# Attention beside a stream of products: factors turned behind the weighted sums, used behind the next minima; operand pieces split a visit after their load

## The chip, the cores and the metric

The kernel runs on one core of a Trainium2 chip. Its metric is the device time in microseconds of one execution of the whole program, from a launch to its end. TensorE (PE) multiplies and turns matrices into PSUM, VectorE (DVE) and ScalarE (ACT) work on tiles elementwise, GpSimd (POOL) does a few elementwise operations and issues stores, and SyncE (SP) issues most of the loads. Each of these runs its own list of instructions in order, and they wait for one another by semaphores.

## The reference, cut to what matters

One decoder layer on 1024 tokens of width 1024, in float32: two branches, a state space model (ssm) and an attention with forgetting, are gated, merged and projected. The part around the change is the attention of 16 heads of 64 columns, and the branch products behind it:

```python
scale = ATT_HEAD_DIM ** -0.5
fcum = jnp.cumsum(log_f, axis=-1)
for blk in range(seqlen // ATT_BLOCK):
    q0, q1 = blk * ATT_BLOCK, (blk + 1) * ATT_BLOCK
    s = jnp.einsum('bhqd,bhkd->bhqk', q[:, :, q0:q1], k[:, :, :q1]).astype(jnp.float32) * scale
    s = s + fcum[:, :, q0:q1, None] - fcum[:, :, None, :q1]
    s = jnp.where(kpos[None, :] <= qpos[:, None], s, -jnp.inf)
    prob = jax.nn.softmax(s, axis=-1)
    outs.append(jnp.einsum('bhqk,bhkd->bhqd', prob.astype(v.dtype), v[:, :, :q1]))
...
y_att = (o.astype(f32) * jax.nn.silu(z_att.astype(f32))).astype(x.dtype)
p_ssm = jnp.einsum('ble,ed->bld', y_ssm, w_branch_ssm)
p_att = jnp.einsum('ble,ed->bld', y_att, w_branch_att)
merged = jax.nn.sigmoid(g_ssm) * p_ssm + jax.nn.sigmoid(g_att) * p_att
out = jnp.einsum('bld,de->ble', merged, w_out)
return x + _rmsnorm(out, post_g)
```

## The kernel before

**The stream of products.** Every large product is a `Pair`: two units of 128 output columns computed by a scheme of seven block products (`do`, numbers 1 to 7). Each block product is one *step* of 12 matmuls (`matmuls`, four pieces of 128 rows by three products of high and low parts) and runs in two halves of six. `Stream.steps` is a list of all steps written out by hand; `half` runs the next half, and three steps ahead prepares the weights' high and low part (`split` in `Pair`: ACT writes the high part, L351, DVE the low part, L352; the tile is `wop`). The results go from PSUM (`pb`, `pc`, `pd`) to SBUF by `keep` (L404) and `give` (L412 to L418).

**Operands.** The moving side of a product is an operand of four pieces, each 128 x 512, in a high and a low part (`x0h`, `x0l` and so on; x0 is `b11`, x1 `b21`, x2 `-b22`, x3 `t1`, x4 `-t2`, x5 `t3`, x6 `t4`). Three sets follow one another in the same tiles: the layer's input at first, then the ssm branch's output (`ops_s`), the attention's output (`ops_a`), and in the end the output weights (`ops_w`). Where a pair is the last that uses a set, each operand is opened for the next set as soon as its step is over (`Stream.half`), and `Operands.some`, called once a half, does two things: it fetches up to two pieces that are ready (L265, SP loads), and it splits up to two pieces that were fetched more than two calls ago (ACT L277 or L280, DVE L278 or L281, both held to the program's order). With a name given (`only`), at a step's start, it splits what that step still lacks. During the second part of a visit's fill the calls are put off (`hold`) and done one after another in the next visit (`release`).

**Attention.** It runs beside the stream in 48 visits, six a pair of heads (`GROUPS`): two query blocks against up to 512 keys. A visit m of the loop from L1599 does, in order:

- `scores`: the products on PE into four score tiles (`s`, one for each head and block), for each a minimum on DVE (L1459, tile `ex`, minimum `nm`) and an exponential with its sum on ACT (L1463), held to this order;
- `weighted`, of the visit before: the weighted sums (`av`) on PE;
- every second visit `free`, which multiplies the sums of the group just ended by its gate and frees the PSUM bank (`o`, L1412);
- `release`, then at a group's end `settle`, which compares the minima of the key halves;
- `fill(m, 0)`: halves of the stream's steps, a share worked out from `rooms` and `weights`;
- at a group's end `scale`, which makes eight factors a query (`ns`), and `load_gates`; `loads` of queries, keys, values and gates for later visits;
- `turned`: the exponentials turned on PE into `pt` and copied to `p` by ACT or DVE;
- `fill(m, 1)`, with the operands' calls put off.

A group of query blocks ends every second visit (g odd; n = 0, 1, 2 in a pair of heads). Its factors lie one query to a row and have to be turned: `send` turns them on PE (`tp`), copies them on ACT (`st`, L1385) and has POOL store them to DRAM in two pieces (`st_dram`, L1387); `take` loads them back with two SP loads, spread over the rows (`rb`, L1393); `out` multiplies by them on DVE (L1424 and the addition L1425, or L1418 alone for n = 2) and calls `outputs`, which has POOL store the result (`ya_dram`, L1514) and make the differences that the scheme of seven needs.

Before the change, a group that ends in visit m is sent in visit m + 1 behind `turned`, taken at the start of visit m + 2 ahead of `fill(m + 2, 0)`, and put out in visit m + 2 behind `turned`. For the last pair of heads, groups 1 and 2 were taken at the end of visit m + 1 and put out ahead of that fill.

**What sets the order.** All of PE's instructions stand as the program has them (`mm`, `turn`), and so do those marked `pin` on the other engines, among them the minima, the exponentials, the operands' splits, the multiplications by factors and POOL's stores. All others, the loads on SP too, are placed among these by a planner that goes by its own estimate of the durations; those under `tc.high_priority()` come first when they can. The score tiles, `pt` and `tp` are all of one tag with four PSUM banks, used in turn: a new tile takes the bank of the fourth last and waits for whoever still reads that.

Of the kernel before, what the change touches and what calls it, by code (L numbers as in the profile page):

```python
# [19 lines left out]
NK = D // P  # L20
# [66 lines left out]
def hybrid_layer(ctx: ExitStack, tc, a, out):  # L87
# [73 lines left out]
    class Operands:  # L161
# [9 lines left out]
        def __init__(self, name, src, there=lambda k, h: True, order=lambda op: op, queue=nc.gpsimd):  # L171
            self.src, self.there, self.order, self.queue = src, there, order, queue
            self.copy = src
            self.tiles, self.left, self.made, self.at, self.step = {}, {}, set(), {}, 0
            self.lows = {}
            self.dram = {n: tc.dram_tile([KH, P, HALF], F32, name=f"{n}_{name}") for n in self.LESS}

# [111 lines left out]
        def put(self, j, **parts):  # L289
            for name, raw in parts.items():  # L290
                self.made.add((name, j))
                name = "-" + name if name in ("t2", "b22") else name
                self.at[name, j] = self.step
                self.split(name, j, raw)

        def some(self, only=None):

            self.step += 1
            n = 0
            for name in list(self.left):  # L300
                for j in list(self.left[name]):
                    if (only is None and n < 2 or name == only) and (name, j) not in self.at:
                        if self.ready(name.strip("-"), j):
                            self.fetch(name, j)
                            self.at[name, j] = self.step
                            n += 1
            n, most = 0, 1 if "merged" in fin else 2
            for name, j in list(self.at):
                if j in self.left[name]:
                    if name == only or only is None and n < most and self.at[name, j] < self.step - 2:  # L310
                        self.split(name, j)
                        n += 1

# [142 lines left out]
    class Stream:  # L456
# [6 lines left out]
        def __init__(self, pairs, double, last):  # L463
            self.pairs = pairs
            for n, p in enumerate(pairs):
                p.bank, p.other = (pj, "be"[n % 2]), (pjx, "d") if n < double else (pj, "c")

                p.between = n < double or n >= last

            p, q, r = pairs[0:3]  # L470
            self.steps = [(p, 1), (q, 1), (p, 2), (q, 2)] + [(p, n) for n in (6, 5, 7, 3, 4)]
            self.steps += [(q, 6), (q, 5), (q, 7), (r, 1), (q, 4), (q, 3)]
            for n in range(2, last):
                p, nxt = pairs[n], pairs[n + 1]
                self.steps += [(p, i) for i in ((2, 6, 5, 7) if n < double else (6, 2, 7, 5))] + [(nxt, 1)]
                self.steps += [(p, 4), (p, 3)] if n + 1 < last else [(p, 3), (p, 4)]

            a, b, c, d, e, f, g, h = pairs[last:]
            self.steps += [(a, 5), (a, 6), (a, 7), (b, 1), (a, 2), (a, 4), (a, 3)]
            for p, nxt in ((b, c), (c, d), (d, e)):  # L480
                self.steps += [(p, 2), (p, 6), (p, 5), (p, 7), (nxt, 1), (p, 4), (p, 3)]
            self.steps += [(f, 1), (e, 2), (e, 6), (e, 5), (e, 7), (f, 2), (e, 4), (e, 3)]
            self.steps += [(f, 6), (f, 5), (f, 7), (g, 1), (f, 4), (f, 3)]
            self.steps += [(g, 2), (g, 6), (g, 5), (g, 7), (h, 1), (g, 4), (g, 3)]
            self.steps += [(h, 6), (h, 5), (h, 7), (h, 2), (h, 3), (h, 4)]
            self.following = {p: n.ops for p, n in zip(pairs, pairs[1:]) if n.ops is not p.ops}
            self.building = []
            self.chores = []
            self.held = None
            self.count = 0  # L490
            self.at = 0
            self.run = None
            self.waiting = []
            self.loads = [(p, names) for p in pairs for names in (("a11", "a12"), ("a21", "a22"))]
            self.loaded = []
            self.load_next()
# [635 lines left out]
    with tc.tile_pool(name="pro", bufs=1, reuse_waits="tile", side="right") as pro, tc.tile_pool(  # L1132
        name="prop", bufs=1, space=PSUM, reuse_waits="tile", side="right"
# [51 lines left out]
        stream = Stream(order + late + ends, len(order) + 1, len(order) + len(late) + 4)  # L1185
# [58 lines left out]
    with tc.tile_pool(name="ssm", bufs=1, reuse_waits="tile", side="right") as sp, tc.tile_pool(  # L1244
        name="ssmp", bufs=1, space=PSUM, reuse_waits="tile", side="right"
# [42 lines left out]
    with tc.tile_pool(name="att", bufs=1, reuse_waits="tile", side="right") as ap, tc.tile_pool(  # L1288
        name="attp", bufs=1, space=PSUM, reuse_waits="tile", side="right"
# [139 lines left out]
        heads = {}  # L1429
# [162 lines left out]
        def fill(m, part):  # L1592
            share = weights[min(m // 6, NK - 1)] * rooms[m % 6][part]
            to = stream.steps.index((ends[4], 6))
            stream.halves(round((2 * (to - stream.at) - (stream.run is not None)) * share / left[0]))
            left[0] -= share

        made = []
        for m in range(6 * NK + 1):  # L1599

            hp, g = divmod(m, 6)
            if not g and hp < NK:
                heads[hp] = Heads(hp)
            if m < 6 * NK:
                for u in range(2):
                    scores(hp, g, u)
            for one in made:
                weighted(*one)
            for hd, which in end(m - 1):
                hd.free(which)  # L1610
            stream.release()
            if m == 6 * NK:
                heads[NK - 1].out(2)
                break
            for hd, which in end(m):
                hd.settle(which)
            for hd, which in end(m - 2):
                if not hd.last or not which:
                    hd.take(which)
                else:  # L1620
                    hd.out(which)
            fill(m, 0)

            for hd, which in end(m):
                hd.scale(which)
                hd.load_gates(which)
            loads(m)
            made = turned(hp, g)
            for hd, which in end(m - 2):
                if not hd.last or not which:  # L1630
                    hd.out(which)
            for hd, which in end(m - 1):
                hd.send(which)
            if m == 6 * NK - 1:
                heads[hp].send(2)
            stream.hold()
            fill(m, 1)
            for hd, which in end(m if m == 6 * NK - 1 else m - 1):
                if hd.last and which:
                    hd.take(which)  # L1640


    fp = ctx.enter_context(tc.tile_pool(name="fin", bufs=1, reuse_waits="tile", side="right"))
# [56 lines left out]
```

## Time and profile before

| | |
|---|---|
| time, median of 3 runs | 1315.51 us (1313.98 to 1316.69) |
| the profiled execution's own time | 1316.03 us |
| its span, first to last instruction | 1314.3 us |
| mean granted clock of TensorE | 0.990 |
| attention stage in the span, scores of the first to the sums of the last visit | about 673 to 1158 us |
| operands of the ssm branch loaded and split | about 934 to 1003 us |
| operands of the attention branch loaded and split, as far as in the attention stage | from about 1096 us |

The profile is one execution as the hardware recorded it. A group of instructions is told by its line, its engine and the names that it writes and reads (`out<-in`), with count, total busy time, mean duration, and the time for which the engine stood idle just before, with what ended that. In a timeline each row has start, duration, engine, line and names; an idle time of the engine just before stands in brackets with its releaser. PEclk is the share of its full clock that TensorE was granted. Where a helper records all matmuls they share the line L130 and all transpositions L133; tiles tell them apart.

### The profile page before, as it was taken

How to read it: one execution, taken by the hardware profiler on the slowest of the kernel's cores; microseconds unless marked ns; L12 is line 12 of the kernel's file. 1: busy time of each engine (PE TensorE's matmuls, PEld its weight loads, DVE VectorE, ACT ScalarE, POOL GpSimd, SP SyncE). 2: the span in 40 equal slices, each digit the busy share in tenths (PEclk: the TensorE clock that was granted, in tenths of full speed). 3: DMA queues.
4: the chain of work that ended last, by engine and by line, in shares of the span. 5: the costliest groups of instructions: out<-in, count | busy, mean ns of one | idle time of the engine just before them, and what ended most of it. 6: DMA issues, size and time to landing. Idle time of an engine off the chain costs nothing.

```text
span 1314.3 us, 21050 instructions
## 1 busy us (share of the span) xinstructions
PE 1264.7 (96%) x7054; PEld 992.0 (75%) x7054; DVE 1017.0 (77%) x1977; ACT 793.3 (60%) x1726; POOL 304.0 (23%) x311
## 2 busy tenths in 40 slices
PE   5899999999999999899999999999989998999997
PEld 4578888788887788688777777777767776678886
DVE  7988888798789879778667667666778666888975
ACT  7645665567556656566556565666667555644754
POOL 4000340024102420133002122222121222346152
PEclk9999999999999999999999999999989998999999
DMA  8232543545364545444564657565677556756933
GB/s 292 60 124 65 157 142 121 197 136 154 125 192 124 147 159 158 125 149 153 169 241 157 208 193 228 194 200 195 215 253 264 193 188 216 235 187 214 366 110 104
DMA packets 154668, 233.59 MB, mean 178 GB/s; under 512 B 17216, under 2 KB 62656, under 8 KB 154560
## 3 DMA queue, kind: packets, MB, share of 16 engines
q1 hardware_dynamic: 142016, 205.53, 48.8%
q0 software_dynamic: 6400, 16.10, 3.2%
q10 hardware_dynamic: 6144, 10.62, 2.1%
q8 instruction: 55, 0.90, 0.3%
q14 instruction: 53, 0.43, 0.1%
HBM read 162.99 MB, written 72.34 MB: 179 GB/s over the span
## 4 chain that ended last, share of the span: by engine, by line
PE 70%; DVE 10%; DMA 7%; ACT 6%; issue 4%; SPq 1%; POOL 0%; ACTq 0%; DVEq 0%
PE pb L130 29%; PE pc L130 16%; PE pd L130 5%; PE av L130 5%; PE s L130 5%; PE pt L133 4%; PE yps L130 2%; DVE wop L352 2%; DMA raw<-in_wu 2%; ACT wop L351 1%; PE tr L133 1%; ACT ex L1463 1%; DVE sum L357 1%; PE st L130 1%; DMA xt<-in_x 1%
## 5 line engine op out<-in xcount | busy, mean ns | idle before, releaser
L352 DVE TENSOR_TENSOR wop<-sum,wop 128x512 fp32r<-128x512 f32 x178 | 143.3, 805 | 56.5 <-ACT wop L351 56.2
L1463 ACT ACTIVATE ex<-ex,nm 128x512 f32<-128x512 f32 (+1 forms) x192 | 116.1, 606 | 91.8 <-DVE nm L1459 90.5
L351 ACT ACTIVATE wop<-sum 128x512 fp32r<-128x512 f32 x178 | 111.3, 626 | 94.8 <-PE pc L130 38.8
L404 ACT ACTIVATE s<-pb 128x512 f32<-128x512 f32 x144 | 85.3, 593 | 105.0 <-PE pb L130 101.2
L130 PE MATMUL pc<-x3h,wop 128*128 128x512 f32 x384 | 131.1, 399 | 2.1 <-ACT wop L351 1.0
L352 DVE TENSOR_TENSOR wop<-raw,wop 128x512 fp32r<-128x512 f32 x146 | 106.8, 733 | 33.4 <-ACT wop L351 33.1
L130 PE MATMUL pb<-x6h,wop 128*128 128x512 f32 x384 | 131.0, 398 | 1.2 <-ACT s L404 1.2
L130 PE MATMUL pb<-x0h,wop 128*128 128x512 f32 x384 | 131.8, 401 | 0.0
L130 PE MATMUL pb<-x4h,wop 128*128 128x512 f32 x384 | 130.3, 396 | 0.8 <-ACT x4h L1178 0.8
L130 PE MATMUL pc<-x2h,wop 128*128 128x512 f32 x384 | 130.4, 398 | 0.1
L130 PE MATMUL pb<-x5h,wop 128*128 128x512 f32 x384 | 129.3, 395 | 0.8 <-ACT s L404 0.7
L1459 DVE CUSTOM_DVE_ANT_0 ex<-s,fb 128x512 f32<-128x512 f32 (+1 forms) x192 | 96.7, 551 | 23.3 <-PE s L130 23.3
L351 ACT ACTIVATE wop<-raw 128x512 fp32r<-128x512 f32 x146 | 90.7, 623 | 15.9 <-PE pc L130 9.9
L130 PE MATMUL pd<-x1h,wop 128*128 128x512 f32 x272 | 91.2, 394 | 0.0
L130 PEld LDWEIGHTS pc<-x3h,wop 128*128 128x128 f32 x384 | 72.8, 190 | 20.8 <-issue 4.2
L213 POOL TENSOR_TENSOR wd<-wd 128x256 f32<-128x256 f32 x32 | 33.3, 1040 | 229.1 <-DMA wd<-in_wo 106.5
L130 PEld LDWEIGHTS pb<-x6h,wop 128*128 128x128 f32 x384 | 72.6, 189 | 18.1 <-ACT s L404 1.7
L130 PEld LDWEIGHTS pb<-x0h,wop 128*128 128x128 f32 x384 | 73.4, 191 | 17.0 <-issue 1.8
L130 PEld LDWEIGHTS pb<-x4h,wop 128*128 128x128 f32 x384 | 72.2, 188 | 18.2 <-issue 2.4
L130 PEld LDWEIGHTS pb<-x5h,wop 128*128 128x128 f32 x384 | 72.1, 188 | 18.1 <-ACT s L404 1.7
L130 PEld LDWEIGHTS pc<-x2h,wop 128*128 128x128 f32 x384 | 72.1, 188 | 17.5 <-issue 2.1
L130 PE MATMUL s<-k,q 64*128 64x512 f32 (+3 forms) x576 | 76.0, 378 | 5.8 <-ACT p L1483 3.3
(310 smaller groups left out, 3006.4 us busy)
## 6 DMA issues: line engine op xcount, KB each, us to landing
raw<-in_wu SPq DMA_DIRECT2D x128, 256.0 KB, 3.7
csb<-cs_dram SPq DMA_DIRECT2D x32, 256.0 KB, 5.0
fb<-f_dram SPq DMA_DIRECT2D x16, 512.0 KB, 6.3
rb<-st_dram SPq DMA_DIRECT2D x48, 128.0 KB, 3.1
wd<-in_wo SPq DMA_DIRECT2D x40, 128.0 KB, 3.2
xt<-in_x SPq DMA_DIRECT2D x8, 512.0 KB, 5.9
gs_dram<-th ACTq DMA_DIRECT2D x16, 256.0 KB, 2.6
qh_dram<-th SPq DMA_DIRECT2D x16, 256.0 KB, 4.9
```

The costliest lines, as they stand in the source:

```text
L130: return tc.keep_in_program_order(nc.tensor.matmul(*args, **kw))
L133: return tc.keep_in_program_order(nc.tensor.transpose(out_, in_, idn))
L213: pin(nc.gpsimd.tensor_tensor(t[out_], t[a_], t[b_], ALU.subtract))
L351: nc.scalar.activation(op[:, 0], src, AF.Copy)
L352: nc.vector.tensor_tensor(op[:, 1], src, op[:, 0], ALU.subtract)
L357: self.adds.tensor_tensor(t, x, y, ALU.add)
L404: nc.scalar.activation(s, ps, AF.Copy)
L1459: nc.vector.tensor_tensor_reduce(o, s[e][:, 0:w], fb[hp, h][:, e, 0:w], 1.0, 3.0e38, ALU.add, ALU.min, nm)
L1463: pin(nc.scalar.activation(o, o, AF.Exp, scale=-1.0, bias=nm, accum_out=hd.at(hd.sm, i, h, e)))
```

## The change

- `send` goes from behind `turned` to behind the weighted sums of the same visit, right after `free`, so on PE the factors' transposition stands behind the last weighted sums of its group.
- `take` goes from the start of visit m + 2 to visit m + 1, behind `turned` and ahead of `fill(m + 1, 1)`.
- `out` goes from behind `turned` of visit m + 2 to behind the scores, minima and exponentials of that visit, ahead of the weighted sums.
- The last pair of heads is no longer treated apart, but for its group 2, which is sent and taken in visit 47 and put out in visit 48 as before.
- The stream knows the number of the visit (0 outside the attention). `Operands.some` splits a fetched piece only in a later visit than that of its fetch, except at the start of the step that needs it.

```diff
@@ class Operands, put
-                self.at[name, j] = self.step
+                self.at[name, j], self.visit[name, j] = self.step, stream.visit
                 self.split(name, j, raw)
@@ class Operands, some
                             self.fetch(name, j)
-                            self.at[name, j] = self.step
+                            self.at[name, j], self.visit[name, j] = self.step, stream.visit
                             n += 1
             n, most = 0, 1 if "merged" in fin else 2
             for name, j in list(self.at):
                 if j in self.left[name]:
-                    if name == only or only is None and n < most and self.at[name, j] < self.step - 2:
+                    if name == only or only is None and n < most and self.at[name, j] < self.step - 2 and (
+                        self.visit[name, j] < stream.visit or not stream.visit
+                    ):
                         self.split(name, j)
                         n += 1
@@ the loop over the visits
         for m in range(6 * NK + 1):
 
+            stream.visit = m + 1
             hp, g = divmod(m, 6)
...
             if m < 6 * NK:
                 for u in range(2):
                     scores(hp, g, u)
+            for hd, which in end(m - 2):
+                hd.out(which)
             for one in made:
                 weighted(*one)
             for hd, which in end(m - 1):
                 hd.free(which)
+                if m < 6 * NK:
+                    hd.send(which)
             stream.release()
             if m == 6 * NK:
                 heads[NK - 1].out(2)
+                stream.visit = 0
                 break
             for hd, which in end(m):
                 hd.settle(which)
-            for hd, which in end(m - 2):
-                if not hd.last or not which:
-                    hd.take(which)
-                else:
-                    hd.out(which)
             fill(m, 0)
 
             for hd, which in end(m):
...
             made = turned(hp, g)
-            for hd, which in end(m - 2):
-                if not hd.last or not which:
-                    hd.out(which)
             for hd, which in end(m - 1):
-                hd.send(which)
+                hd.take(which)
             if m == 6 * NK - 1:
                 heads[hp].send(2)
             stream.hold()
             fill(m, 1)
-            for hd, which in end(m if m == 6 * NK - 1 else m - 1):
-                if hd.last and which:
-                    hd.take(which)
+            if m == 6 * NK - 1:
+                heads[hp].take(2)
```

More of the change, by code (lines that the diff above doesn't have):

```diff
@@ L174, in __init__ @@
             self.tiles, self.left, self.made, self.at, self.step = {}, {}, set(), {}, 0
+            self.visit = {}
             self.lows = {}
@@ L490, in __init__ @@
             self.count = 0
+            self.visit = 0
             self.at = 0
```

## The prediction

> **What bounds the kernel now.** I read the page first: engine shares, clock, chain of waits.
>
> ```profile
> span 1314.3 us, 21050 instructions
> ...
> PE 1264.7 (96%) x7054; PEld 992.0 (75%) x7054; DVE 1017.0 (77%) x1977; ACT 793.3 (60%) x1726; POOL 304.0 (23%) x311
> ...
> PEclk9999999999999999999999999999989998999999
> ...
> PE 70%; DVE 10%; DMA 7%; ACT 6%; issue 4%; SPq 1%; POOL 0%; ACTq 0%; DVEq 0%
> ```
>
> PE's matmuls stand in the order of the program and fill 96% of the span, so only two things can be won: PE's idle time, and time at a lower granted clock. Two slices of the clock row show an 8, both in the attention stage. The table of windows, cut where the clock changes, prices them; its columns are length, busy time of PE, PEld, DVE, ACT, POOL, then the clock.
>
> ```profile
> 668.00:960.00 292.00, 288.38 (x1945) 218.75 (x1944) 199.66 (x509) 183.33 (x458) 59.04 (x76) 1.00 0.61 201
> ...
> 973.50:983.80 10.30, 8.80 (x34) 6.19 (x36) 9.29 (x17) 8.44 (x19) 1.50 (x3) 0.52 0.42 158
> ...
> 1103.20:1110.10 6.90, 6.62 (x29) 4.04 (x30) 4.19 (x13) 5.18 (x15) 1.15 (x2) 0.53 0.56 189
> ```
>
> At about half clock the two short stretches lost 10.30 x 0.48 = 4.9 us and 6.90 x 0.47 = 3.2 us. The timeline of PE, DVE and ACT shows what went ahead of each. **Stall A**, in the ssm operands' part:
>
> ```profile
> 966.71 0.69 DVE L1424 TENSOR_TENSOR o<-o,rb 128x512 f32<-128x512 f32 x1 [4.06 <-DMA rb<-st_dram]
> ...
> 970.24 0.72 ACT L1463 ACTIVATE ex<-ex,nm 128x512 f32<-128x512 f32 x1 [6.03 <-DVE nm L1459]
> ...
> 971.11 0.33 PE L133 MATMUL pt<-ident,ex 128*128 128x128 f32 x1 [0.67 <-ACT ex L1463]
> 971.82 0.33 PE L133 MATMUL pt<-ident,ex 128*128 128x128 f32 x1 [0.38 <-ACT ex L1463]
> 973.00 0.40 PE L133 MATMUL pt<-ident,ex 128*128 128x128 f32 x1 [0.85 <-ACT ex L1463]
> 973.60 2.61 PE L133 MATMUL pt<-ident,ex 128*128 128x128 f32 x11 [0.20 <-ACT ex L1463]
> ...
> 977.61 0.38 PE L133 MATMUL tp<-ident,ns 128*8 128x128 f32 x1 [1.40 <-DVE p L1481]
> ```
>
> DVE, in order, stands 4.06 us before the multiplication by the factors (rb), and the next visit's minima stand behind it; ACT's exponentials wait 6.03 us for them, PE's transpositions for those. PE's gaps: 0.67 + 0.38 + 0.85 + 0.20 + 1.40 = 3.5 us. **Stall B**:
>
> ```profile
> 1098.49 0.27 PE L133 MATMUL tp<-ident,ns 128*8 128x128 f32 x1 [0.49 <-DVE p L1481]
> ...
> 1100.62 0.63 ACT L280 ACTIVATE x0h<-x0l 128x512 fp32r<-128x512 f32 x1 [3.50 <-DMA x0l<-ya_dram]
> ...
> 1102.85 1.34 ACT L1483 ACTIVATE p<-pt 128x512 f32<-128x512 f32 x3
> ...
> 1103.47 3.42 PE L130 MATMUL s<-k,q 64*128 64x512 f32 x12 [3.33 <-ACT p L1483]
> ```
>
> ACT stands 3.50 us before a piece whose load is still under way; the copies of p come behind it and PE's scores behind them: 0.49 + 3.33 = 3.8 us. What the whole stage (668 to 1170) holds is in the groups by line, the last number being the engine's idle time before them:
>
> ```profile
> L130 PE MATMUL s<-k,q 64*128 64x512 f32 (+3 forms) x576 | 76.0, 378 | 5.8 <-ACT p L1483 3.3 <-DVE p L1481 2.5
> ...
> L133 PE MATMUL pt<-ident,ex 128*128 128x128 f32 x576 | 74.8, 277 | 5.4 <-ACT ex L1463 5.4
> ...
> L133 PE MATMUL tp<-ident,ns 128*8 128x128 f32 x24 | 6.7, 277 | 4.4 <-ACT p L1483 2.2 <-DVE p L1481 1.9
> ...
> L1424 DVE TENSOR_TENSOR o<-o,rb 128x512 f32<-128x512 f32 x16 | 11.4, 715 | 11.7 <-DMA rb<-st_dram 11.7
> ...
> L280 ACT ACTIVATE x3h<-x3l 128x512 fp32r<-128x512 f32 x8 | 4.7, 620 | 2.5 <-DMA x3l<-t_a 2.5
> ...
> L280 ACT ACTIVATE x5h<-x5l 128x512 fp32r<-128x512 f32 x7 | 4.1, 621 | 1.6 <-DMA x5l<-t_a 1.6
> ```
>
> **The change part by part.** No instruction is added or removed.
>
> *The factors' transposition.* It used to stand right behind the 6 to 16 transpositions of p and took the first of their PSUM banks, so PE waited for the copy just begun: 4.4 us. Now it stands behind the weighted sums, and by the ring of four banks takes that of the visit's first score tile: PE waits for the first minimum on DVE instead, and behind it in PE's order stands the stream's next product. Two visits show this new wait from both sides; in each the rows are the scores' start, the weighted sums, the first minimum:
>
> ```profile
> 713.09 0.96 PE L130 MATMUL s<-k,q 64*128 64x512 f32 x6
> ...
> 714.81 1.95 PE L130 MATMUL av<-p,v 128*64 128x256 f32 x16
> ...
> 714.22 0.69 DVE L1459 CUSTOM_DVE_ANT_0 ex<-s,fb 128x512 f32<-128x512 f32 x1 [1.04 <-PE s L130]
> ...
> 733.59 0.87 PE L130 MATMUL av<-p,v 128*64 128x256 f32 x8
> ...
> 732.99 0.69 DVE L1424 TENSOR_TENSOR o<-o,rb 128x512 f32<-128x512 f32 x1 [2.02 <-DMA rb<-st_dram]
> ...
> 736.81 0.68 DVE L1459 CUSTOM_DVE_ANT_0 ex<-s,fb 128x512 f32<-128x512 f32 x1
> ...
> 1139.86 1.95 PE L130 MATMUL av<-p,v 128*64 128x256 f32 x16
> ...
> 1141.56 0.68 DVE L1459 CUSTOM_DVE_ANT_0 ex<-s,fb 128x512 f32<-128x512 f32 x1
> ```
>
> In the first the minimum ends at 714.91, 1.85 us ahead of the sums' end at 716.76: no wait. In the second it would be 737.49 against 734.46: 3.0 us. Of the 23 visits that turn factors early, nine have the minimum last; the first is this one (3.0), the last that at 1139.86 (0.4), and they sum to 12.9 us. But the four largest (10.3 of it, A's visit with 4.0 among them) follow a wait for rb like the 2.02 us here, which the change moves away; 2.6 us are of other origin. Bounds: 0 and 12.9 us; I take 3.5, near the 2.6 that no rb causes, the four being left with some backlog.
>
> *Store and load of the factors, and their use.* ACT's copy and POOL's two stores go ahead of the visit's first fill; SP's two loads go from the start of the next visit to behind the transpositions of this one; DVE's multiplication and addition (about 0.7 + 0.4 us) and POOL's outputs go from behind the transpositions to behind the minima. The stores' and the loads' landings:
>
> ```profile
> L1385 ACT ACTIVATE st<-tp 8x128 f32<-8x128 f32 x24 | 6.0, 252 | 0.1
> ...
> DMA to landing us min/median/max: 1.6/2.6/5.3
> ...
> DMA to landing us min/median/max: 2.7/3.1/7.0
> ...
> 696.28 1.95 PE L130 MATMUL av<-p,v 128*64 128x256 f32 x16
> ...
> 706.27 0.69 DVE L1459 CUSTOM_DVE_ANT_0 ex<-s,fb 128x512 f32<-128x512 f32 x1
> ...
> SPq L1393 <- DMA st_dram<-st: 68.1, 18, 8.7
> ...
> POOL ms_dram L1060 <- DVE th L1059: 55.0, 11, 9.5
> ```
>
> With two issues of some 0.55 us on each queue, the way from copy to factors is 0.85 + 2.6 + 0.6 + 3.1 = 7.2 us. In the tightest pair of visits (groups 2 and 3) the sums end at 698.2, the copy, between exponentials, at 699.0 to 699.9 (estimate); factors at 706.2 to 707.1; the minima end at 706.96. So at the medians DVE waits about 0.1 us; with both slowest landings 6.7 us. Other pairs have more room, and the pair that produced A gains it: now its use comes behind minima, so a late load holds up splits and gives of the same visit, no longer the next minima. SP already waits 68.1 us for these stores, in order, and later loads behind them; this stays. Cover: DVE is idle 32% of the first window, some 3.2 us a visit of 10. Below: nothing; above: rival 3. I take 1.
>
> *Pieces taken up a visit later.* Their loads stay; ACT's 0.62 us and DVE's 0.69 us of each move. B's cause goes, as do the 2.5 and 1.6 us for x3 and x5. An operand has some six products (two to four visits) between reload and use, so a visit's delay is hidden; without that cover PE would wait about 1.3 us a piece at a product's start. Bunched behind the exponentials, four pieces are 2.5 us of ACT, before p's copies: I put 1.5 us for one such lateness.
>
> **The sum.** A: 3.5 + 4.9 = 8.4. B: 3.8 + 3.2 = 7.1. Other waits of tp: 4.4 - 1.40 - 0.49 = 2.5. Other waits of pt: 5.4 - 2.1 = 3.3, half of it (1.6) since the rest is the stage's start. Other waits of s: 5.8 - 3.3 = 2.5, half (1.2). Together 20.8; less 3.5 + 1 + 1.5 = 6 leaves 14.8 us. The profiled execution took 1316.0 us by the clock of the runs (1.7 around its span), 0.5 over their median 1315.5: 1316.0 - 14.8 = 1301.2, and 1301 beside that median.
>
> The Trainium skill, "TensorE: Matmul & The Clock Gate", Part 1, has the clock halve after an idle window of about 3.4 us. A's rows differ: gaps of at most 0.85 us, 2.1 us in all, went ahead of the 0.52. By the rule a new 3 us wait of tp would cost 3 us alone; by A's rows up to 4.9 more. The sum stays, as A's loss is measured.
>
> **Rivals.**
> 1. *One stall survives* (20%): rb still lands late where operand loads crowd the queues, or the pieces bunch. For it: 7.0 us as the slowest landing was A's own. Against: A's wait now has a visit's other work behind it. Then one of A and B, some 8 us, stays: 1309.
> 2. *Lateness only moves* (11%): DVE and ACT have as much to do, the planner puts the free operations elsewhere, and new gaps, with half clock after them, cost about the 15 us: 1315.
> 3. *Slower* (13%): POOL runs its queue in order, and a store of the factors behind a store that waits for DVE (up to 9.5 us) comes late; rb then lands late, and DVE stands behind the minima with splits, gives and copies of p queued behind it. It decides where that wait passes DVE's 3.2 us of idle time a visit; at 4.7 us in the 16 visits with little room (groups 3 and 5) it is 1.5 x 16 = 24 us, against 20.8 - 5 = 16 won otherwise: 1316 + 8 = 1324. Against: POOL mostly stood waiting for these very copies.
>
> **How the numbers follow.** Forecast 1301 with 56%, 1296 to 1306 by itself (costs of 1 to 11). The range must take in rival 1 and most of 2: 1295 to 1317, which leaves out rival 3 and a little below. A measurement tells about 0.2% (2.6 us) from no change: faster 0.76 (forecast and rival 1), same 0.11, slower 0.13.
>
> **What would show it.** Right: PE's clock 1.00 from 668 to 1157, tp's idle time below 3.5, no ACT wait of x0h for its load, o<-o,rb waits short and followed by no wait of PE. Wrong: PE idle before tp by DVE's minima; long waits for rb right behind minima; PE waiting at a product's start for a split; a half-clock stretch at a new place.

## The result, and the profile after

| | before | after |
|---|---|---|
| median, five runs each | 1315.51 us (1313.98 to 1318.54) | 1306.57 us (1304.39 to 1308.89) |
| the profiled execution, its span | 1316.03, 1314.3 us | 1308.89, 1307.2 us |
| ratio of the times, 95% interval | | 0.9929 (0.991 to 0.9949) |

The change makes the kernel 8.9 us faster, 0.7%, clear of the 0.2% that a measurement can tell. The forecast was 1301; the time lies in its range, on its side, and about 6 us of the 14.8 are missing.

First the page of the kernel after, the same lines as before: shares of the span, and the clock in 40 slices.

```profile
span 1307.2 us, 21069 instructions
...
PE 1258.4 (96%) x7054; PEld 988.5 (76%) x7054; DVE 1016.9 (78%) x1977; ACT 794.5 (61%) x1726; POOL 301.3 (23%) x311
...
PEclk9999999999999999999999999999999999999999
```

As many matmuls, and no slice of the clock under 9 any more. PE's busy time fell by 6.3 us (1264.7 to 1258.4) without one matmul less: the same matmuls take less time, as they do at full clock. The table of windows has it by place (length, then PE, PEld, DVE, ACT, POOL, then clock, DMA share, GB/s). Before:

```profile
960.00:1080.00 120.00, 114.98 (x733) 86.03 (x732) 87.94 (x221) 74.12 (x183) 24.15 (x35) 0.96 0.68 227
1080.00:1170.00 90.00, 82.31 (x511) 61.34 (x509) 66.89 (x155) 55.09 (x133) 24.62 (x32) 0.96 0.64 213
```

After, with the three windows of the stage and one short stretch in the first of them:

```profile
668.00:960.00 292.00, 286.00 (x1915) 217.32 (x1913) 198.85 (x499) 181.62 (x448) 58.36 (x76) 0.99 0.61 199
960.00:1080.00 120.00, 115.63 (x779) 87.36 (x776) 96.03 (x233) 78.43 (x196) 25.61 (x37) 1.00 0.68 235
1080.00:1170.00 90.00, 85.64 (x539) 65.00 (x538) 75.27 (x164) 56.37 (x134) 32.40 (x35) 1.00 0.69 232
...
718.10:721.50 3.40, 3.40 (x22) 1.89 (x20) 1.93 (x8) 2.72 (x8) 0.00 (x0) 0.50 0.23 77
```

The two windows that held stalls A and B are at full clock and hold more matmuls. The first window, at 1.00 before, is at 0.99: there is a half-clock stretch at 718 that was not there. What stood ahead of PE in the whole stage, in the groups by line (busy time, mean ns, idle time just before and what ended it):

```profile
L130 PE MATMUL s<-k,q 64*128 64x512 f32 (+3 forms) x576 | 74.8, 369 | 7.2 <-DVE p L1485 5.3 <-ACT p L1487 1.6
...
L133 PE MATMUL pt<-ident,ex 128*128 128x128 f32 x576 | 71.9, 273 | 3.0 <-ACT ex L1467 3.0
...
L133 PE MATMUL tp<-ident,ns 128*8 128x128 f32 x24 | 6.6, 273 | 2.5 <-DVE nm L1463 1.4 <-DVE ns L1381 1.1
```

Transpositions of p (pt) wait 3.0 us and not 5.4, those of the factors (tp) 2.5 and not 4.4; the scores (s) wait **more**, 7.2 and not 5.8, and 5.3 of it for DVE's copies of p. The largest of these gaps ends at 716.64, 1.5 us ahead of the half-clock stretch. The timelines of POOL, SP, DVE and PE show how it comes about (in brackets the idle time before and its releaser):

```profile
700.95 1.33 POOL L1391 DMA_DIRECT2D st_dram<-st  x2 [6.71 <-ACT st L1389]
...
707.47 1.13 SPq L1397 DMA_DIRECT2D rb<-st_dram  x2
...
711.67 0.69 DVE L1428 TENSOR_TENSOR o<-o,rb 128x512 f32<-128x512 f32 x1 [3.68 <-DMA rb<-st_dram]
...
715.90 0.68 DVE L1485 COPY p<-pt 128x512 f32<-128x512 f32 x1
716.64 0.96 PE L130 MATMUL s<-k,q 64*128 64x512 f32 x6 [2.51 <-DVE p L1485]
```

Read it from the end. PE wants its next scores, whose bank a piece of `pt` still holds; DVE copies that piece only at 715.90, since it stands in order behind the multiplication by the factors (rb) and a dozen other operations; DVE had stood 3.68 us before that multiplication; SP had issued the loads only at 707.47, for they wait for POOL's stores, issued from 700.95. From there to the factors it took 10.7 us, where the medians have 7.2 from the copy on. This is the new wait: **no longer the next minima stand behind a late factor, but the next copies of p.** Over the kernel DVE waits for rb in the rows

```profile
DVE o L1428 <- DMA rb<-st_dram: 11.3, 8, 3.7
...
DVE zr L1422 <- DMA rb<-st_dram: 2.6, 2, 1.6
```

(total, times, longest), 13.9 us in ten waits, more than the 11.7 before.

To split the gain I take the attention stage from the first scores to the start of the second product behind the last weighted sums (the first that uses x5), in each profiled execution. PE's gaps and its time at half clock in it are added up from the timeline and the clock; half of the half-clock time is lost. PE's gap right ahead of that product, 0.69 us in both, is not counted.

| | stage | PE idle in it | at half clock |
|---|---|---|---|
| before | 489.1 us | 15.7 | 17.1 |
| after | 480.1 us | 14.0 | 3.4 |

Of the stage's 9.0 us, (17.1 - 3.4) / 2 = 6.8 are clock and 1.7 are gaps. The stage starts 0.9 us later and what follows it takes 1.0 us more: 9.0 - 1.9 = 7.1, the difference between the two profiled executions. So in this pair the change won mainly the clock back that two chains of gaps had cost, while the gaps themselves hardly got fewer. The runs of both kernels in the experiments below say the same, less sharply: their mean granted clock goes from 0.991 to 0.995, and 0.004 of 1310 us is about 5 of the 9 to 11 us won; PE's gaps are 12.2 and 13.2 us in two further profiles of the changed kernel.

### The profile page after: what moved, and what is told of

It reads as the page before. It is cut to its first block, busy times and chain, and to the rows that moved or that the text cites. A ratio compares the mean times of both kernels' runs of the same rounds, so it can differ in the third digit from the quotient of the medians.

```text
span 1307.2 us, 21069 instructions
## 1 busy us (share of the span) xinstructions
PE 1258.4 (96%) x7054; PEld 988.5 (76%) x7054; DVE 1016.9 (78%) x1977; ACT 794.5 (61%) x1726; POOL 301.3 (23%) x311
## 5 line engine op out<-in xcount | busy, mean ns | idle before, releaser
L355 DVE TENSOR_TENSOR wop<-sum,wop 128x512 fp32r<-128x512 f32 x178 | 140.5, 790 | 57.9 <-ACT wop L354 57.2
L355 DVE TENSOR_TENSOR wop<-raw,wop 128x512 fp32r<-128x512 f32 x146 | 103.2, 707 | 33.6 <-ACT wop L354 33.0
L354 ACT ACTIVATE wop<-raw 128x512 fp32r<-128x512 f32 x146 | 90.8, 623 | 17.7 <-PE pc L130 10.6
L130 PEld LDWEIGHTS pb<-x0h,wop 128*128 128x128 f32 x384 | 73.4, 191 | 15.6 <-issue 0.5
```

The lines of the kernel that those rows point to most:

```text
L130: return tc.keep_in_program_order(nc.tensor.matmul(*args, **kw))
L354: nc.scalar.activation(op[:, 0], src, AF.Copy)
L355: nc.vector.tensor_tensor(op[:, 1], src, op[:, 0], ALU.subtract)
```

## The experiments

Three questions were open. Which of the two parts, the new order of the factors or the later splits, brings what? Is the rest the wait for rb that the use behind the minima sets up, or the late transposition? And is it POOL's stores that come late? The results, each beside the kernel before on the same chip (its median 1313.79 in the first four rows, 1314.31 in the next four, 1315.18 in the last four); the last columns are from one profiled execution each, with the stage bounded as above (PE's gap right ahead of its end is 0.69 us in all but act_store, 1.66, and split_act_store, 1.57):

| kernel | median us | ratio (95%) | stage | PE idle | at half clock | DVE waits for rb |
|---|---|---|---|---|---|---|
| order_only | 1308.40 | 0.996 (0.9944 to 0.9975) | 484.6 | 15.6 | 10.2 | 17.5 |
| split_only | 1320.90 | 1.0052 (1.0031 to 1.0073) | 491.4 | 20.7 | 17.0 | 15.1 |
| out_late | 1308.97 | 0.9969 (0.9954 to 0.9985) | 481.6 | 17.0 | 6.8 | 1.5 |
| act_store | 1310.54 | 0.9988 (0.997 to 1.0006) | 484.4 | 13.4 | 13.7 | 5.3 |
| after_again | 1303.44 | 0.9915 (0.9894 to 0.9937) | 477.3 | 12.2 | 0 | 16.1 |
| out_mid | 1301.29 | 0.9899 (0.9875 to 0.9922) | 474.4 | 10.6 | 3.4 | 1.3 |
| split_act_store | 1303.12 | 0.9905 (0.988 to 0.9929) | 477.5 | 9.0 | 6.8 | 2.2 |
| mid_act_store | 1306.33 | 0.9941 (0.9919 to 0.9962) | 479.5 | 11.9 | 10.2 | 0.6 |
| store_only | 1308.61 | 0.9954 (0.9933 to 0.9975) | 479.8 | 12.3 | 3.4 | 2.8 |
| mid_order | 1306.06 | 0.9932 (0.9914 to 0.9951) | 475.5 | 10.6 | 3.4 | 4.5 |
| after_third | 1305.24 | 0.9925 (0.9903 to 0.9947) | 477.9 | 13.2 | 0 | 15.1 |
| out_mid_again | 1301.64 | 0.9899 (0.9878 to 0.992) | 473.3 | 11.5 | 0 | 1.4 |

### order_only: the new order of the factors alone

The changed kernel with the old condition for a split:

```diff
-                    if name == only or only is None and n < most and self.at[name, j] < self.step - 2 and (
-                        self.visit[name, j] < stream.visit or not stream.visit
-                    ):
+                    if name == only or only is None and n < most and self.at[name, j] < self.step - 2:
```

> The new order of send, take and out alone, with the pieces' splits as before. If the two halves of the change act on separate stalls (theory), stall A and the waits of the factors' transposition go and stall B stays: of the 9 us that the whole change won some 7 are given back, so about 1313 us beside 1315.5, with ACT again waiting over 3 us for x0's load near 1100 and a stretch at half clock behind it. If B was only lateness handed on by the factors (rival), B does not come back and the time is that of the whole change, 1306 to 1307.

The ratio is 0.996: this part alone wins 5.4 us, more than was expected. Stall B is back, though smaller. In the timelines of ACT and PE the lines of this kernel have numbers smaller by 2: the copies of p are L1483 on DVE and L1485 on ACT.

```profile
1098.27 0.63 ACT L281 ACTIVATE x0h<-x0l 128x512 fp32r<-128x512 f32 x1 [1.82 <-DMA x0l<-ya_dram]
...
1099.96 1.71 PE L130 MATMUL s<-k,q 64*128 64x512 f32 x11 [1.54 <-ACT p L1485]
```

1.54 us where it had been 3.33, and the window from 1095 to 1110 has a clock of 1.00. So the unlanded piece is B's cause, and PE's wait goes with ACT's: 1.82 us of ACT gave 1.54 here, 3.50 gave 3.33 before the change, and 2.21 gives 1.96 in store_only below. At A's place PE still waits 2.17 us for the factors' transposition (969.16), with a step at half clock behind it. The late copies of p are there as in the changed kernel (DVE waits 17.5 us for rb); the timeline has

```profile
712.77 0.96 PE L130 MATMUL s<-k,q 64*128 64x512 f32 x6 [2.14 <-DVE p L1483]
```

and the windows a half-clock stretch behind it:

```profile
714.00:717.40 3.40, 3.40 (x24) 1.91 (x22) 2.16 (x8) 2.72 (x8) 0.00 (x0) 0.54 0.24 77
```

### split_only: the later splits alone

The kernel before with the edits of the change in `Operands` and the stream's count of visits, nothing else:

```diff
-                    if name == only or only is None and n < most and self.at[name, j] < self.step - 2:
+                    if name == only or only is None and n < most and self.at[name, j] < self.step - 2 and (
+                        self.visit[name, j] < stream.visit or not stream.visit
+                    ):
```

> The splits a visit after their fetch alone, with send, take and out as before. Theory: B goes, A stays with its half clock near 973, the waits of the factors' transposition stay at 4 us: about 1308 to 1310. Rival (B is no cause of its own): no change, 1315.

This missed: 0.52% **slower** than the kernel before. B is gone (0.17 us left there), A is larger (gaps of 3.70, 0.32 and 1.99 us), and the end of the stage has a new stall. The timelines of ACT, POOL, DVE and PE:

```profile
974.59 0.39 PE L133 MATMUL pt<-ident,ex 128*128 128x128 f32 x1 [3.70 <-ACT ex L1467]
...
1144.23 0.25 ACT L1389 ACTIVATE st<-tp 8x128 f32<-8x128 f32 x1
...
1147.25 0.58 POOL L1064 DMA_DIRECT2D ms_dram<-th  x1 [8.77 <-DVE th L1063]
1147.84 1.14 POOL L1391 DMA_DIRECT2D st_dram<-st  x2
...
1156.59 0.69 DVE L1428 TENSOR_TENSOR o<-o,rb 128x512 f32<-128x512 f32 x1 [3.56 <-DMA rb<-st_dram]
...
1159.17 0.63 ACT L278 ACTIVATE x4h<-x 128x512 fp32r<-128x512 f32 x1 [3.75 <-DVE x L1530]
...
1159.85 0.50 PE L130 MATMUL pb<-x4h,wop 128*128 128x512 f32 x1 [2.70 <-ACT x4h L278]
1163.87 0.80 PE L130 MATMUL pb<-x4l,wop 128*128 128x512 f32 x1 [3.52 <-DVE x4l L279]
```

The last pair's factors were copied at 1144.23 to 1144.48, but POOL's queue stood 8.77 us before another store (ms_dram) that waited for DVE. So their stores went out at 1147.84, 3.4 us late; DVE waited 3.56 us for them; the difference that makes x4 came behind, ACT's split behind that, and the stream's product behind that: 2.70 + 3.52 us of PE, with half clock from 1162.5 to 1169.3 in the bargain. This is the mechanism of the prediction's rival 3, one store behind another in POOL's queue, but under the **old** order of the factors. In the kernel before, the same stores went out 0.29 us behind the copy; that the later splits moved DVE's work by enough to make the other store late is inferred. In the changed kernel, where the factors are sent a fill earlier, POOL issues them at most 0.30 us behind the copy. The two parts are therefore not to be added up: -0.40% and +0.52% alone, -0.71% together.

### out_late: the use of the factors behind the transpositions again

```diff
             for hd, which in end(m - 2):
-                hd.out(which)
+                if hd.last and which:
+                    hd.out(which)
...
             made = turned(hp, g)
+            for hd, which in end(m - 2):
+                if not hd.last or not which:
+                    hd.out(which)
```

> The whole change, but the factors are used where they were before, behind the transpositions of p (the last pair of heads as in the change). Theory: what the change fell short of is DVE standing before factors that have not landed, 13.9 us in ten waits, two of 3.7 us that handed 2.5 and 0.7 us on to PE and brought a half-clock stretch; with half a visit more for the landing these waits fall below 3 us in all, the half clock near 716 goes, and the time is 1301 to 1304. Rival (the late copies of p on DVE come from the bunched work, not from the factors): PE's waits for DVE's copies stay near 5 us, 1306 to 1308, or more, since use now stands ahead of the next minima again.

DVE's waits for rb fell as expected, from 13.9 to 1.5 us, and PE's gap behind the first of them is gone: so the place of the use makes that gap. But the expected time was missed: 1308.97, no better than the changed kernel, for the wait went to the place where the prediction had priced it and then let it off:

```profile
L133 PE MATMUL tp<-ident,ns 128*8 128x128 f32 x24 | 6.6, 277 | 10.3 <-DVE nm L1463 7.3 <-DVE ns L1381 3.0
```

10.3 us of PE ahead of the factors' transposition, not 2.5: 7.3 for the first minimum on DVE, 3.0 for the factors (ns) themselves. With the use behind the transpositions DVE reaches that minimum late, though it hardly waits for rb any more. (In the prediction's tally of the old trace the sum over the visits was 12.9 us.) Four of these waits, 5.2 us together, come behind one operation of DVE that takes 1.68 to 2.17 us where the rows beside it take 0.68. Each time GpSimd starts an operation of its own beside it, which its queue holds behind the store of the result that the use has just made, as at the first of them:

```profile
730.73 2.17 DVE L355 TENSOR_TENSOR wop<-raw,wop 128x512 fp32r<-128x512 f32 x1
...
731.04 1.30 POOL L214 TENSOR_TENSOR x<-x,th 128x512 f32<-128x512 f32 x1
```

That POOL's operation held up DVE's is read from this overlap; no run tests it. One place makes the copies of p late, the other the minima.

### act_store: the factors' stores on ACT's queue

```diff
-                    pin(nc.gpsimd.dma_start(st_dram[self.hp, n, :, 256 * h : 256 * h + 256], st[4 * h : 4 * h + 4, :]))
+                    pin(nc.scalar.dma_start(st_dram[self.hp, n, :, 256 * h : 256 * h + 256], st[4 * h : 4 * h + 4, :]))
```

> The whole change, but ACT issues the two stores of the factors in place of POOL. Theory: POOL's stores took up to 7.0 us to land, and that is why factors come late; from ACT's hardware queue they land in about 3 us, DVE's waits for rb fall from 13.9 to under 6 us, and the time falls to 1302 to 1305. Rival (the landing is set by the loads under way at that time, whoever issues): waits stay above 10 us and the time within 2 us of the whole change; two more issues in ACT's order cost it up to 1 us a group.

Missed: the waits for rb fell to 5.3 us, as the theory of POOL's stores has it (how fast the stores land from ACT's queue the trace doesn't tell), but the kernel is slower than the changed one (0.9988 against 0.9929 to 0.9915). At the place of the longest wait DVE and PE have:

```profile
710.39 1.23 DVE L1377 TENSOR_TENSOR sm<-sm 128x4 f32<-128x4 f32 x1
...
711.95 0.68 DVE L1485 COPY p<-pt 128x512 f32<-128x512 f32 x1
...
712.68 0.96 PE L130 MATMUL s<-k,q 64*128 64x512 f32 x6 [2.25 <-DVE p L1485]
```

The copy of p came 4.0 us earlier (711.95 for 715.90), but PE was ready for it earlier too (712.68 - 2.25 = 710.43, for 716.64 - 2.51 = 714.13), so its gap is nearly what it was; part of that is an operation of 4 columns that took 1.23 us (0.15 in the changed kernel), beside one of POOL's from 710.18 to 711.60. The stage has 13.7 us at half clock in four stretches, at 714, 977, 1001 and 1148. Shortening the way of the factors alone was therefore not enough.

### out_mid: the use between the two

It stands behind the visit's first half of fill, ahead of `loads` and `turned`: behind the minima as in the changed kernel, and later by a fill, but still ahead of the copies of p and of the next minima.

```diff
             for hd, which in end(m - 2):
-                hd.out(which)
+                if hd.last and which:
+                    hd.out(which)
...
                 hd.load_gates(which)
+            for hd, which in end(m - 2):
+                if not hd.last or not which:
+                    hd.out(which)
             loads(m)
```

> The whole change, but the factors are used behind the visit's first fill and ahead of the transpositions of p, between the change's place (behind the minima) and the old one (behind the transpositions). Theory: at the change's place DVE waits 13.9 us for factors, at the old place it waits 1.5 us but the use stands ahead of the next minima and PE's factor transposition waits some 10 us for these; in the middle both fall, the waits for rb below 5 us and those of the transposition below 4, and the time is 2 to 4 us under the changed kernel. Rival (the stalls are wherever DVE's total work leaves no room): the sum of PE's idle time stays, time within 2 us of the changed kernel.

1301.29 us beside 1303.44 for the changed kernel in the same comparison. DVE's waits for rb are down to

```profile
DVE zr L1422 <- DMA rb<-st_dram: 1.1, 1, 1.1
...
DVE o L1428 <- DMA rb<-st_dram: 0.2, 1, 0.2
```

and PE's rows are

```profile
L130 PE MATMUL s<-k,q 64*128 64x512 f32 (+3 forms) x576 | 73.5, 368 | 3.9 <-DVE p L1485 2.3 <-ACT p L1487 1.6
L133 PE MATMUL pt<-ident,ex 128*128 128x128 f32 x576 | 71.8, 273 | 2.9 <-ACT ex L1467 2.9
L133 PE MATMUL tp<-ident,ns 128*8 128x128 f32 x24 | 6.6, 276 | 3.0 <-DVE nm L1463 2.5 <-DVE ns L1381 0.5
```

The scores wait 3.9 us and not 7.2, and the transposition of the factors hardly more than in the changed kernel. The stores are as slow as there, as the last line of the factors' tile shows, first for out_mid:

```profile
DMA to landing us min/median/max: 1.6/3.1/6.9
```

then for the changed kernel:

```profile
DMA to landing us min/median/max: 1.6/3.3/6.9
```

So it is the **place of the waiting instruction** in DVE's order that decides, not the landing as such. The largest gap left is one of 2.25 us ahead of the factors' transposition at A's place (966.19).

### after_again, after_third, out_mid_again: the same kernels once more

> The changed kernel as it is, beside the variants that follow: it gives the same ratio to before as in its first timing, 0.991 to 0.995.

> The changed kernel once more, as the control for the next one: 0.991 to 0.993 of before.

> The use in the middle once more: 2 us under the changed kernel if its first result was no accident; if it was, the same as the changed kernel within 1 us.

The changed kernel gave 0.9929, 0.9915 and 0.9925 in three comparisons, with a stage of 480.1, 477.3 and 477.9 us. The gap ahead of those scores is in all three profiles (2.51, 2.17 and 1.95 us), and DVE's wait for rb ahead of it is 3.68, 3.34 and 3.09: each time the gap is the wait less 1.14 to 1.17, and in order_only too (2.14 for 3.29). The half-clock stretch behind it is in the first alone, and that hangs on where the gap falls. In every profile the half-clock stretches start on a grid of 3.413 us (in the changed kernel at 52.53, 554.29 and 718.13, that is 147 and 48 steps apart). In the first profile one step took 1.92 us of the gap, and the next step was at half clock (length, PE, PEld, DVE, ACT, POOL, then the clock):

```profile
714.72:718.13 3.41, 1.49 (x16) 1.03 (x16) 2.76 (x8) 2.03 (x5) 0.00 (x0) 1.00 0.20 77
```

In after_again a step's end at 715.68 cut the gap into 1.06 and 1.11 us, as one at 712.94 did in after_third, and the clock stayed:

```profile
712.27:715.68 3.41, 2.35 (x15) 1.75 (x13) 3.41 (x11) 2.09 (x5) 0.00 (x0) 1.00 0.50 163
715.68:719.09 3.41, 2.30 (x26) 1.58 (x28) 2.76 (x8) 1.66 (x4) 0.00 (x0) 1.00 0.20 77
```

So these 1.7 us of lost clock are bad luck of the first profile, not a cost of every execution.

out_mid gave 0.9899 twice. In each comparison the two intervals overlap, so 2.2 and 3.6 us between the medians are not certain singly; both have the same sign, and the stage shows the same 3 to 5 us. PE's idle time and half clock carry only a part of that: after_third and out_mid_again have no half clock, and of the 4.5 us between their stages 1.7 are idle time. The rest is time that the profile counts as PE's busy time; what holds it was not followed.

### split_act_store and store_only: the stores on ACT's queue under the old order

split_act_store is split_only with the edit of act_store; store_only is the kernel before with that edit, one word.

> The later splits alone, with the two stores of the factors issued by ACT in place of POOL. Theory: what made the later splits alone slower than before was the last pair of heads, whose factors lay 3.6 us in POOL's queue behind a store of the ssm product that waited for DVE; PE then stood 2.7 and 3.5 us before the last piece of x4, at half clock behind it. From ACT's queue these waits near 1160 go, stall A stays: some 8 to 10 us under the later splits alone, 1310 to 1313. Rival (the bunched splits themselves are what is late there): the waits before x4 stay, and the time is 1318 or more.

> The kernel before, with nothing changed but that ACT issues the two stores of the factors in place of POOL. Theory: the wait for rb behind stall A and the waits in the other tight visits (11.7 us in all) come from the way of the factors, and POOL is part of it; they fall below 4 us, stall A shrinks and B stays: 1306 to 1310 beside 1314. Rival (the later splits alone carry what the pair of both edits won): no change, 1312 or more.

split_act_store: 1303.12, that is 17.8 us less than split_only. (The two stand in different comparisons; by the ratios it is 1.5%.) The waits before x4 are gone, so POOL's queue was the cause of that stall; and A shrank to one gap, with one step at half clock behind it, which had not been expected:

```profile
970.06 0.27 PE L133 MATMUL tp<-ident,ns 128*8 128x128 f32 x1 [2.18 <-ACT p L1487]
```

store_only came out as expected, 0.9954: the waits for rb go from 11.7 to 2.8 us. A keeps gaps of 3.3 us, at other places, but 3.4 us of half clock instead of 10.2; B stays, being another thing, with gaps of 2.4 us instead of 3.8 and no half clock:

```profile
1096.77 0.63 ACT L280 ACTIVATE x0h<-x0l 128x512 fp32r<-128x512 f32 x1 [2.21 <-DMA x0l<-ya_dram]
...
1099.55 2.15 PE L130 MATMUL s<-k,q 64*128 64x512 f32 x12 [1.96 <-ACT p L1483]
```

One word thus wins more than half of what the change wins, and with the later splits (split_act_store) about as much as the whole change, with the factors' order untouched.

### mid_act_store: out_mid with the stores on ACT's queue

> The factors used in the middle, and stored by ACT. Theory: if both are right, waits for rb below 2 us and those of the transposition below 4, the lowest time of all, 1300 to 1304. Rival: the two issues in ACT's order delay the exponentials and copies, and it is no better than the use in the middle alone.

This missed: 1306.33, 5 us **slower** than out_mid in the same comparison. There is no wait for rb left to win, and the stage has 10.2 us at half clock instead of 3.4. Each of the two issues takes some 0.58 us of ACT's queue, ahead of its exponentials and copies. That these cause the new stretches was argued only; no run isolates it, and the same stays open for act_store.

### mid_order: out_mid with the old condition for a split

> The order with the use in the middle, and the splits as before. Theory: the splits are worth here what B costs there, a wait of ACT before x0 handed on to the scores: 3 to 6 us over the use in the middle with the later splits. Rival (with the better order B has no price): within 2 us of it.

1306.06, 4.4 us over out_mid in the same comparison, as expected: with the new order in its better place the later splits are still worth having.

## Why the prediction came out as it did

The mechanism was right: in all three profiles of the changed kernel both stalls are gone, and so is the half clock behind them. At A's place that was narrow: PE's new wait for the factors' transposition is 0.94 us there, but 2.17 in order_only, 2.20 in out_late, 2.26 in mid_act_store and 2.73 in mid_order, each with a step at half clock, though all four send the factors at the same place. The sizes, term by term from the three rows of PE's idle time and the stretches at half clock, with the new waits of tp taken as their own term:

| term | predicted | measured |
|---|---|---|
| stall A with its half clock | 8.4 | 6.9 |
| stall B with its half clock | 7.1 | 7.1 |
| other old waits of tp | 2.5 | 2.5 |
| other waits of pt | 1.6 | 0.3 |
| other waits of s | 1.2 | -3.2 |
| new waits of tp | -3.5 | -2.5 |
| rb behind the minima, beyond what s shows | -1 | 0 |
| a new half-clock stretch | 0 | -1.7 |
| pieces split later, and other products | -1.5 | -1.4 |
| sum | 14.8 | 8.0 |

The stage shortened by 9.0 us by its own ends, so some 1 us is in no row; the medians differ by 8.9. Against 14.8 the two terms of the scores' waits and their clock lack 6.1, A and pt another 2.8; tp and rb's own term give 2.0 back.

- **A.** Half clock and the five old gaps are gone, as expected. (The prediction puts all of the first four, 2.1 us, ahead of the half clock. It set in at 973.12, so the 0.20 us ahead of 973.60 lie behind that, and 1.90 went ahead.) What is left at its place is 0.93 + 0.23 + 0.29 us ahead of scores (two of these for ACT's copies of p) and a new wait of tp of 0.94, which stands in its own row:

```profile
969.40 0.79 PE L130 MATMUL s<-k,q 64*128 64x384 f32 x6 [0.93 <-DVE p L1485]
...
972.06 0.27 PE L133 MATMUL tp<-ident,ns 128*8 128x128 f32 x1 [0.94 <-DVE nm L1463]
```

- **B** went altogether; mid_order and order_only bring it back, in part. At its place the copies of p now come first and the pieces behind them, without a wait:

```profile
1096.63 1.35 ACT L1487 ACTIVATE p<-pt 128x512 f32<-128x512 f32 x3
...
1102.97 1.14 ACT L281 ACTIVATE x0h<-x0l 128x512 fp32r<-128x512 f32 x2
```

- **The factors' transposition** was priced at 3.5 from a range of 0 to 12.9, on the reason that a use ahead of the minima causes most of the 12.9. It cost 2.5, and out_late, with the use ahead of the minima again, 10.3: the range holds, and the place of the use is what costs. But the prediction named a late rb as the reason, and in out_late DVE waits for rb only 1.5 us; the use itself and an operation held up beside POOL's do it there. That 2.5 came so near to 3.5 is in part luck, since 1.1 of it is a wait for the factors (ns) on DVE that the prediction doesn't name.
- **The step that failed is the wait for rb**: "at the medians DVE waits about 0.1 us", "now its use comes behind minima, so a late load holds up splits and gives of the same visit, no longer the next minima", "I take 1". The first half was seen (the tightest pair, groups 2 and 3, does have one of the two longest waits, 3.68 us), and the upper end of 6.7 was never reached. But three things were left out. The median is not what decides: the slow landings of the stores, up to 6.9 us, come in just where there is least room. And the landings were taken from the old trace, a median of 2.6 and at most 5.3; in the changed kernel the same stores take 3.3 and 6.9, why is open. And behind splits and gives stand the copies of p, whose bank the next scores want; the idle time of DVE was counted as cover, though it lies elsewhere in the visit. So this term, with "other waits of s" of which I had half saved, came to 3.2 us more of gaps and 1.7 of half clock, together a loss of 4.9, instead of a gain of 1.2 less 1. The gap of 2.51 and the half clock behind it, 4.2 us, are the late rb's. The rest are smaller gaps, most of them with no wait for rb ahead; the largest, 1.09 at 1129.88, comes behind a wait of DVE for another load (th, 1.90 us), and a like one of 1.26 stood in the old stage at 1139.01, so that half of these would go was a guess that failed. Moving the use by one fill (out_mid) takes the waits for rb from 13.9, 16.1 and 15.1 us to 1.3 and 1.4, and the time to the 1301 that had been forecast for the change; that it is the same number is chance, since out_mid is another order.
- **Rival 3** (POOL's queue) did not happen in the changed kernel: its stores were issued within 0.30 us of the copy. It did happen in split_only, at 1147.
- **Pieces split later** mostly had their cover. ACT's waits of 2.5 and 1.6 us for x3 and x5 are down to 0.3 and gone; one product waited 0.73 us for a low part, another 0.66 for a copy that DVE, late with a factor, gave late:

```profile
889.85 0.50 PE L130 MATMUL pc<-x3h,wop 128*128 128x512 f32 x1 [0.66 <-DVE th L417]
...
1148.86 0.50 PE L130 MATMUL pc<-x3l,wop 128*128 128x512 f32 x1 [0.73 <-DVE x3l L282]
```

- **Waits of pt** were a guess at half; 1.5 us of the 3.0 left are the stage's start, and the two others, 0.38 and 1.12, came up at new places.

## What to carry to other kernels

Ask of every instruction that waits for a transfer which instruction behind it in its engine's order is wanted first, and move the waiting one until the transfer's slow landings fit ahead of it, not its median; moving it too far makes the next thing late, so try the places between. Two edits that each shift an in-order queue should be run alone and together, since one may mend or make the other's stall. A small store on which a chain depends should not share a queue with stores that wait for something else; that one edit gave more than half of this change's gain, and cost time where it was no longer needed.

## What the runs showed of the hardware

- A store of 2 KB landed between 1.6 and 6.9 us after its issue in the changed kernel (median 3.3), and between 1.6 and 5.3 in the kernel before (median 2.6). The slow landing of rb behind stall A, 7.0 us before the change, fell where the DMA engines were full, a share of 0.99, as the window of the kernel before shows:

```profile
958.00:967.00 9.00, 9.00 (x64) 6.70 (x61) 3.87 (x12) 5.56 (x16) 0.00 (x0) 1.00 0.99 299
```

  For the stores issued at 700.95 no such cause was found, the share being 0.73 from 700.9 to 707.5; this stays open.
- The clock was halved behind single gaps of 2.51 us (716.64 in the changed kernel) and 2.14 us (712.77 in order_only), and in the kernel before behind gaps of at most 0.85 us, 1.90 in all. It was not halved behind a gap of 2.17 us at the same place in after_again, whose timeline has

```profile
716.79 0.96 PE L130 MATMUL s<-k,q 64*128 64x512 f32 x6 [2.17 <-DVE p L1485]
```

  nor behind one of 2.25 us in out_mid:

```profile
966.19 0.27 PE L133 MATMUL tp<-ident,ns 128*8 128x128 f32 x1 [2.25 <-DVE nm L1463]
```

  The stretches themselves are 3.41 us or two or three times that (6.83, 10.24), but for the last, which the program's end cuts off, and they start on a grid of that step. From 650 to about 1178 us of all 14 profiles, no step at full clock with less than 1.17 us of PE's idle time in it was followed by half clock, 11 of the 25 with 1.17 to 1.92 us were, and all 12 with more. The gaps of 2.17 and 2.25 us each lay across the end of a step and left at most 1.38 us in one. The Trainium skill, "TensorE: Matmul & The Clock Gate", Part 1, has the clock halve after an idle window of about 3.4 us. The step of the grid agrees; as the length of one gap, or as a window idle from end to end, the rows contradict it. What else decides between 1.17 and 1.92 us stays open.
